# Hymba encoder block on one core: other tile places at the end of each up stage, and an addition of the second up stage held behind a weight split

## The chip, the cores and the metric

The kernel runs on one core of one Trainium2 chip. The metric is the device time of one execution in microseconds (us). The engines have these names: PE is TensorE (matmuls; PEld its weight loads), ACT is ScalarE, DVE is VectorE, POOL is GpSimd and SP is SyncE. POOL and SP mostly issue transfers here, each into a queue of its own.

## The reference

A layer of an encoder over 2,048 tokens and 16 learned meta tokens, width 1,024, all in float32. An attention group and a Fourier group stand side by side, then comes an MLP, then a last norm:

```
h = concat(meta, x)
hn = rms_norm(h, g_mix); proj = hn @ w_in
mixed = concat(rms_norm(attention(q, k, v)), rms_norm(fourier_mix(u)))
h = h + mixed @ w_out
m = rms_norm(h, g_mlp)
h = h + square(relu(m @ w_up)) @ w_down        # w_up 1024 x 4096, w_down 4096 x 1024
return rms_norm(h, g_final)[:, n_meta:]
```

The change touches the MLP alone, the last two lines but one.

## The kernel before, in words

**Splitting.** Every float32 matrix goes to TensorE as two parts in the type fp32r: a high part, a cast on ACT (L70), and a low part, source minus high part, on DVE (L71). Together they are called a split. A product takes three matmuls of 128x512 (`mm3`, L80 to L82): high by high, high by low, low by high.

**Seven forms.** The MLP's two products are done in 2x2 blocks with seven block products in place of eight, named by digits and done in the order 1, 2, 6, 5, 7, 3, 4. Some operands are sums or differences of blocks, which DVE works out. Results of several forms are added up into the blocks of the product.

**Two passes, two stages each.** The tokens are taken in two passes, p = 0 and p = 1. Each pass has an up stage (`up_pass`) and a down stage (`down_pass`).

- Up stage: eight groups g of 512 hidden columns; for each, seven forms of 24 matmuls into two banks each. The activation parts are the tiles `bf` (in the first pass made in place, in the second read back from memory, 2 MB for a form: L1616, L1622). The raw weights are `R0` and `R1`, their sums `us1` and `us2` (L1138, L1139, L1144), their parts `wuh` and `wul`. After form 2, ACT has copied form 1's result out (`p1`, L1248) and DVE adds the two halves `c11` (L1259); ACT then applies relu and square (L1212, L1213). The results and their sums `s1` to `s4` are stored to memory, `s_d`, from SP's queue (L1219).
- Down stage: four groups of seven forms of 48 matmuls. The stored results come back as raws `a` (L1351), the weights w_down as raws `d11`, `d21`, `d12`, `d22` (L1332); in the first group both are issued by POOL. DVE works out the sums of weights (L1372: `d11`, `t2` and so on). Parts of activations are `ah`, `al`, parts of weights `bh`, `bl`. Form 1's parts for the first group (`a1p`, `bh1`, `bl1`, `ah1`, `al1`) are made in the up stage, by `first_down`. Results lie in four banks `dx` and four banks `dy`; DVE adds them to the residual `hs` (L1493). Form 6 writes into the `dx` banks again, after form 1's additions have read them.

**What sets the order.** TensorE's order is the order of the code. For the other engines a layer that records the program sets it, mostly in the order in which inputs are there; `tc.issue_after(x)` puts what it encloses behind instruction x. Every wait comes from the data or from addresses: SBUF is shared out by pools at the left and the right end (`dn` left and `dr` right for the down stage, `pc` and `sp` right in the up stage, `bfb` left in the second up stage). A pool takes the addresses of one that was released, and with `reuse_waits="tile"` a new tile waits for exactly those instructions that still read or write the old tile at its place. `place` sets in which order the tags of a pool take their addresses. `own2` makes the parts of form 2 in places of their own, `ah0` to `bl1`; all other parts take turns in rings, "a" in `dn` and "b" in `dr`.

At the end of the up stage `sp` is released after form 1's matmuls are in the queue, and `dr` lies where it was, so over the tiles `R0`, `us1`, `us2`, which hold form 1's parts at that time:

```
if "b" not in RING:
    sp.release()
    if final_pass:
        wup.release()
    dr = right(f"dr{p}")
    RING["b"] = dr, b_bufs
    place(dr, ("b", 1024, b_bufs))
    own2("b", 0)
```

Of the kernel before, what the change touches and what calls it, by code (L numbers as in the profile page):

```python
# [12 lines left out]
R32 = mybir.dt.float32r  # L13
AF = mybir.ActivationFunctionType
ALU = mybir.AluOpType
# [4 lines left out]
P = 128  # L20
# [64 lines left out]
def ins_of(x):  # L85
    return getattr(x, "ins", x)
# [49 lines left out]
def encoder_block(ctx: ExitStack, tc: tile.TileContext, x, meta, w_in, w_f,  # L136
                  w_out, w_up, w_down, g_fin, g_cols, g_rows, c_id, c_rope, c_dft, c_even, c_odd, c_rem, out):
    nc = tc.nc
    split = Split(nc)
    x = x[0]  # L140
# [451 lines left out]
    for j in range(LAST + 1):  # L592
# [16 lines left out]
        else:  # L609
# [14 lines left out]
            a = 0  # L624
# [578 lines left out]
                load(*items[at + 1])  # L1203
            yield

    def up_pass(p, sp, pc, UW, ready, first, hs, beside):

        def c_tile(name):
            return pc.tile([P, 512], F32, name=f"{name}_{p}", tag="c", bufs=11)
# [5 lines left out]
        for g in range(8):  # L1215
# [5 lines left out]
            for name in ORDER:  # L1221
# [21 lines left out]
                for q in range(2):  # L1243
                    nm = f"{g}_{q}"
                    if name in "165":
                        d = p1 if name == "1" else u2 if name == "6" else p5
                        d[q] = pc.tile([P, 512], F32, name=f"p{name}_{p}_{nm}", tag="p", bufs=P_BUFS)
                        nc.scalar.copy(d[q], (Y if name == "5" else X)[q])  # L1248
                    elif name == "4":
                        C["21", q] = c = c_tile("c21_" + nm)  # L1250
                        relu2(c, X[q])
                        keep("2", q, c)
                        s4 = c_tile("s4_" + nm)
                        nc.vector.tensor_tensor(s4, c, C["s2", q], op=ALU.subtract)
                        keep("3", q, s4)
                    else:
                        f, a, b = {"2": ("11", Y, p1), "7": ("22", X, p5), "3": ("12", Y, u2)}[name]
                        C[f, q] = c = c_tile(f"c{f}_{nm}")
                        nc.vector.tensor_tensor(c, a[q], b[q], op=ALU.add)  # L1259
                        relu2(c, c)  # L1260
                        if name != "3":
                            keep("1" if name == "2" else "4", q, c)
                        else:
                            s1, s2, s3 = (c_tile(f"s{i}_{nm}") for i in (1, 2, 3))
                            nc.vector.tensor_tensor(s1, c, C["22", q], op=ALU.add)
                            keep("5", q, s1)
                            nc.vector.tensor_tensor(s2, s1, C["11", q], op=ALU.subtract)
                            keep("6", q, s2)
                            C["s2", q] = s2
                            nc.vector.tensor_tensor(s3, C["11", q], c, op=ALU.subtract)  # L1270
                            keep("7", q, s3)
# [32 lines left out]
    def down_pass(p, sp, FIRST, hs):  # L1304

        dn = left(f"dn{p}")
        final_pass = p == 1
        own, RING = {}, {"a": (dn, 8)}
        a_bufs, b_bufs = (5, 10) if p else (4, 8)

        def place(pool, *tags):

            for tag, cols, bufs in tags:
                pool.tile([P, cols], F32, name=f"z{tag}_{p}", tag=tag, bufs=bufs)

        raws_ = {n: (n, 1024, 2) for n in ("d11", "d21", "d12", "d22", "t2")}
        ends_ = [(n, 512, 1) for n in ("gf0", "gf1", "ej0", "ej1")]
        own_ = [(n, 1024, 1) for n in ("ah0", "al0", "ah1", "al1")]
        if p:
            place(dn, *ends_, *(raws_[n] for n in ("t2", "d21", "d11")), ("ar", 1024, a_bufs), *own_,  # L1320
                  raws_["d12"], raws_["d22"], ("a", 1024, 8))
        else:
            place(dn, raws_["d11"], raws_["d21"], ("ar", 1024, a_bufs), *own_, raws_["d12"], raws_["d22"], raws_["t2"],
                  ("a", 1024, 8), *ends_)

        def load(raw, g, i, j):
            raw[i, j] = []
# [7 lines left out]
        def own2(x, g):  # L1335

            for h in range(2):
                own[g, x, h] = [RING[x][0].tile([P, 2, 512], R32, name=f"{x}{e}2_{p}_{g}_{h}", tag=f"{x}{e}{h}")
                                for e in "hl"]

        def down_operands():
# [87 lines left out]
        ready = [next(DO)]  # L1429
# [42 lines left out]
        for g in range(4):  # L1472
            X, Y = {}, {}
            last = g == 3
            for name in ORDER:
# [36 lines left out]
                if not (last and name == "4"):  # L1512
                    for t in range(4):
                        products(t)
# [3 lines that stand above are left out]
                            wup.release()  # L1518
                        dr = right(f"dr{p}")
                        RING["b"] = dr, b_bufs  # L1520
                        place(dr, ("b", 1024, b_bufs))
                        own2("b", 0)
                        ready.append(next(DO))
                    w = next(DO, None)
                    if w is not None:
# [28 lines left out]
    sp = right("sp0")  # L1554
    UW = up_weights(0, sp, sp)
    ready = [next(UW), next(UW)]
# [42 lines left out]
    pc = right("pc0")  # L1599
    hs, FIRST = [], []  # L1600
# [5 lines left out]
    ready = down_pass(0, sp, FIRST, hs)  # L1606
    sp = right("sp1")
    spr = left("spr1")
    UW = up_weights(1, sp, spr)
# [7 lines left out]
    for name in "2U65734":  # L1617
        with tc.issue_after(ins_of(behind)):
            if name == "U":
                ready.append(next(UW))  # L1620
            else:
                behind = nc.sync.dma_start(f32v(BT[name]), f_d[name])  # L1622
    pc = right("pc1")
    hs, FIRST = [], []
    up_pass(1, sp, pc, UW, ready, first_down(1, FIRST, sp), hs, iter(()))
    pc.release()
    bfb.release()
    spr.release()
# [103 lines left out]
```

## Time and profile before

| | |
|---|---|
| median of 3 runs | 2271.43 us (2271.02 to 2275.55) |
| profiled execution | 2272.19 us |
| its span, first to last instruction | 2270.4 us |
| mean granted TensorE clock | 0.997 |
| PE busy | 2240.4 us, 99% |
| DVE busy | 1693.0 us, 75% |
| ACT busy | 1177.8 us, 52% |

In the rows of the profile "dx<-bh,ah" names the written tile and the read ones by the program's names, with the numbers of form and group left out; where several tiles share a line, the first name stands for all (the row "c<-uy,p" is the addition at L1259). In brackets stands how long the engine had stood idle just before the instruction and what ended that. A row of the timeline is: start, duration (or, for a group of "xN" instructions in a row, their time together), engine, line, operation. Matmul times overlap: one starts about every 0.227 us and lasts 0.39. The first down stage begins at 1332.07 us, the second up stage at 1641.7, the second down stage at 1954.22.

### The profile page before, as it was taken

The numbers are of one execution on the slowest core, as the hardware profiler recorded it, in microseconds if no ns is written. First come the engines' busy times: TensorE is split into PE (matmuls) and PEld (weight loads), VectorE is DVE, ScalarE is ACT, GpSimd is POOL, SyncE is SP. The second block draws the span as 40 slices with busy tenths as digits, with TensorE's granted clock in tenths as the row PEclk, the third lists the DMA queues.
The fourth block names the chain that finished last, engine by engine and source line by source line (L and its number), as shares of the span: only waits on it lengthen the run. The fifth ranks groups of instructions, "written<-read, shape, count | busy, mean of one in ns | idle before, by whom it ended". The sixth has DMA issues, their size and how long they took to land.

```text
span 2270.4 us, 28121 instructions
## 1 busy us (share of the span) xinstructions
PE 2240.4 (99%) x10238; PEld 1774.5 (78%) x10238; DVE 1693.0 (75%) x2250; ACT 1177.8 (52%) x1997; POOL 248.0 (11%) x285
## 2 busy tenths in 40 slices
PE   9999999999999999999999999999999999999998
PEld 7888987766667666677888878888878888788887
DVE  6334589999999888888676669679655656696795
ACT  6443366665555566668555644334445555443343
POOL 2212120003223122010000020000200000200000
PEclk9999999999999999999999999999999999999999
DMA  5332252133343524367777575444674444864442
GB/s 203 89 107 77 78 157 81 51 94 113 101 155 116 192 90 136 126 254 243 254 233 237 201 275 192 158 133 149 227 311 166 156 151 155 306 201 157 128 138 84
DMA packets 191786, 367.40 MB, mean 162 GB/s; under 512 B 15760, under 2 KB 74768, under 8 KB 189984
## 3 DMA queue, kind: packets, MB, share of 16 engines
q1 hardware_dynamic: 171040, 310.08, 40.4%
q0 software_dynamic: 20464, 55.27, 7.7%
q8 instruction: 80, 1.31, 0.2%
q14 instruction: 58, 0.48, 0.1%
q10 hardware_dynamic: 144, 0.26, 0.0%
HBM read 236.28 MB, written 129.27 MB: 161 GB/s over the span
## 4 chain that ended last, share of the span: by engine, by line
PE 88%; DVE 7%; ACT 2%; issue 2%; POOL 1%; DMA 1%; POOLq 0%; DVEq 0%; ACTq 0%; SPq 0%
PE o L849 7%; PE ux L82 5%; PE ux L80 5%; PE ux L81 5%; PE dx L80 5%; PE dx L81 5%; PE dx L82 5%; PE uy L82 4%; PE uy L81 4%; PE uy L80 4%; PE dy L82 4%; PE dy L80 4%; PE dy L81 4%; PE s L80 2%; PE s L82 2%; PE s L81 2%
## 5 line engine op out<-in xcount | busy, mean ns | idle before, releaser
L849 PE MATMUL o<-S,vn 128*128 128x512 f32 x512 | 243.6, 596 | 4.2 <-ACT S L841 3.5
L70 ACT CAST ah<-a 128x1024 fp32r<-128x1024 f32 x108 | 112.9, 1050 | 259.8 <-PE dx L81 105.3
L80 PE MATMUL dx<-bh,ah 128*128 128x512 f32 x496 | 192.6, 388 | 1.3 <-DVE hs L1493 1.3
L780 ACT COPY S<-s 128x512 f32<-128x512 f32 x256 | 145.0, 584 | 91.9 <-PE s L82 72.5
L82 PE MATMUL dx<-bh,al 128*128 128x512 f32 x496 | 192.5, 388 | 0.0
L81 PE MATMUL dx<-bl,ah 128*128 128x512 f32 x496 | 192.5, 388 | 0.0
L80 PE MATMUL ux<-bf,wuh 128*128 128x512 f32 x448 | 176.0, 393 | 3.2 <-ACT wuh L70 3.1
L82 PE MATMUL ux<-bf,wul 128*128 128x512 f32 x448 | 175.4, 392 | 0.7 <-DVE wul L71 0.7
L81 PE MATMUL ux<-bf,wuh 128*128 128x512 f32 x448 | 175.4, 391 | 0.0
L840 DVE TENSOR_TENSOR S<-S,mb 128x1024 f32<-128x1024 f32 x128 | 155.2, 1227 | 11.8 <-ACT mb L811 11.7
L841 ACT ACTIVATE S<-S 128x1024 f32<-128x1024 f32 x128 | 135.1, 1063 | 43.3 <-DVE S L840 42.2
L80 PE MATMUL dy<-bh,ah 128*128 128x512 f32 (+1 forms) x388 | 151.5, 390 | 3.5 <-ACT ah L70 3.5
L82 PE MATMUL dy<-bh,al 128*128 128x512 f32 (+1 forms) x388 | 151.3, 390 | 1.6 <-DVE al L71 1.6
L71 DVE TENSOR_TENSOR al<-a,ah 128x1024 fp32r<-128x1024 f32 x108 | 131.1, 1220 | 27.2 <-ACT ah L70 26.9
L81 PE MATMUL dy<-bl,ah 128*128 128x512 f32 (+1 forms) x388 | 151.2, 390 | 0.0
L849 PEld LDWEIGHTS o<-S,vn 128*128 128x128 f32 x512 | 92.2, 189 | 75.1 <-issue 59.0
L80 PE MATMUL s<-q,kt 128*128 128x512 f32 (+1 forms) x272 | 145.1, 534 | 2.8 <-ACT S L780 2.4
L71 DVE TENSOR_TENSOR bl<-d,bh 128x1024 fp32r<-128x1024 f32 x92 | 112.1, 1219 | 21.5 <-ACT bh L70 21.5
L80 PE MATMUL uy<-bf,wuh 128*128 128x512 f32 x320 | 125.0, 391 | 0.3 <-ACT wuh L70 0.3
L82 PE MATMUL uy<-bf,wul 128*128 128x512 f32 x320 | 124.6, 390 | 0.7 <-DVE wul L71 0.7
L786 DVE TENSOR_TENSOR M<-M,S 128x1024 f32<-128x1024 f32 x96 | 117.6, 1225 | 9.9 <-ACT S L780 9.0
L81 PE MATMUL uy<-bf,wuh 128*128 128x512 f32 x320 | 124.8, 390 | 0.0
(323 smaller groups left out, 5663.2 us busy)
## 6 DMA issues: line engine op xcount, KB each, us to landing
a<-s_d SPq DMA_DIRECT2D x84, 512.0 KB, 3.7
R<-in_w_up_dram SPq DMA_DIRECT2D x32, 1024.0 KB, 5.5
s_d<-s SPq DMA_DIRECT2D x128, 256.0 KB, 2.1
s_d<-c SPq DMA_DIRECT2D x96, 256.0 KB, 2.8
d<-in_w_down_dram SPq DMA_DIRECT2D x48, 512.0 KB, 5.1
f_d<-lf SPq DMA_DIRECT2D x56, 256.0 KB, 2.8
bf<-f_d SPq DMA_DIRECT2D x7, 2048.0 KB, 13.5
a<-s_d POOLq DMA_DIRECT2D x24, 512.0 KB, 5.3
```

What stands on the lines that cost most here:

```text
L70: self.high = nc.scalar.copy(hi, src)
L71: self.low = nc.vector.tensor_tensor(lo, src, f32v(hi), op=ALU.subtract)
L80: nc.tensor.matmul(out, a[0], b[0], start=first, stop=False, skip_group_check=chain)
L81: nc.tensor.matmul(out, a[0], b[1], start=False, stop=False, skip_group_check=chain)
L82: nc.tensor.matmul(out, a[1], b[0], start=False, stop=last, skip_group_check=chain)
L780: nc.scalar.copy(S[:, i % 2], ps)
L786: nc.vector.tensor_tensor(M, M, S, op=ALU.max)
L840: nc.vector.tensor_tensor(S, S, mb, op=ALU.subtract)
L841: nc.scalar.activation(p, S, AF.Exp, scale=ISQ)
L849: nc.tensor.matmul(s["O"], v[:, 2 * j % 4 + e], p[:, e], start=i + e == 1, stop=False)
```

## The change

Three edits, with no instruction added or removed.

1. **Own places of form 2's weight parts** (`bh0`, `bl0`, `bh1`, `bl1`). In the second pass they move from `dr` to `dn`, behind `d22` and ahead of the ring "a". In the first pass they stay in `dr`, but take its first addresses, ahead of the ring "b".
2. **First pass, order in `dn`:** the ring "a" takes its addresses ahead of `d12`, `d22` and `t2`, no longer behind them.
3. **Second pass, first group:** the additions of `c11` after form 2 are issued behind the split of form 6's weights (`held`).

```diff
--- before.py
+++ after.py
@@ -1203,7 +1203,7 @@
                 load(*items[at + 1])
             yield
 
-    def up_pass(p, sp, pc, UW, ready, first, hs, beside):
+    def up_pass(p, sp, pc, UW, ready, first, hs, beside, held=None):
 
         def c_tile(name):
             return pc.tile([P, 512], F32, name=f"{name}_{p}", tag="c", bufs=11)
@@ -1256,7 +1256,8 @@
                     else:
                         f, a, b = {"2": ("11", Y, p1), "7": ("22", X, p5), "3": ("12", Y, u2)}[name]
                         C[f, q] = c = c_tile(f"c{f}_{nm}")
-                        nc.vector.tensor_tensor(c, a[q], b[q], op=ALU.add)
+                        with tc.issue_after(held) if held is not None and (g, name) == (0, "2") else nullcontext():
+                            nc.vector.tensor_tensor(c, a[q], b[q], op=ALU.add)
                         relu2(c, c)
                         if name != "3":
                             keep("1" if name == "2" else "4", q, c)
@@ -1316,12 +1317,13 @@
         raws_ = {n: (n, 1024, 2) for n in ("d11", "d21", "d12", "d22", "t2")}
         ends_ = [(n, 512, 1) for n in ("gf0", "gf1", "ej0", "ej1")]
         own_ = [(n, 1024, 1) for n in ("ah0", "al0", "ah1", "al1")]
+        ownb_ = [(n, 1024, 1) for n in ("bh0", "bl0", "bh1", "bl1")]
         if p:
             place(dn, *ends_, *(raws_[n] for n in ("t2", "d21", "d11")), ("ar", 1024, a_bufs), *own_,
-                  raws_["d12"], raws_["d22"], ("a", 1024, 8))
+                  raws_["d12"], raws_["d22"], *ownb_, ("a", 1024, 8))
         else:
-            place(dn, raws_["d11"], raws_["d21"], ("ar", 1024, a_bufs), *own_, raws_["d12"], raws_["d22"], raws_["t2"],
-                  ("a", 1024, 8), *ends_)
+            place(dn, raws_["d11"], raws_["d21"], ("ar", 1024, a_bufs), *own_, ("a", 1024, 8), raws_["d12"],
+                  raws_["d22"], raws_["t2"], *ends_)
 
         def load(raw, g, i, j):
             raw[i, j] = []
@@ -1335,7 +1337,7 @@
         def own2(x, g):
 
             for h in range(2):
-                own[g, x, h] = [RING[x][0].tile([P, 2, 512], R32, name=f"{x}{e}2_{p}_{g}_{h}", tag=f"{x}{e}{h}")
+                own[g, x, h] = [(dn if final_pass else RING[x][0]).tile([P, 2, 512], R32, name=f"{x}{e}2_{p}_{g}_{h}", tag=f"{x}{e}{h}")
                                 for e in "hl"]
 
         def down_operands():
@@ -1518,8 +1520,8 @@
                             wup.release()
                         dr = right(f"dr{p}")
                         RING["b"] = dr, b_bufs
+                        own2("b", 0)
                         place(dr, ("b", 1024, b_bufs))
-                        own2("b", 0)
                         ready.append(next(DO))
                     w = next(DO, None)
                     if w is not None:
@@ -1618,11 +1620,12 @@
         with tc.issue_after(ins_of(behind)):
             if name == "U":
                 ready.append(next(UW))
+                held = ins_of(split.low)
             else:
                 behind = nc.sync.dma_start(f32v(BT[name]), f_d[name])
     pc = right("pc1")
     hs, FIRST = [], []
-    up_pass(1, sp, pc, UW, ready, first_down(1, FIRST, sp), hs, iter(()))
+    up_pass(1, sp, pc, UW, ready, first_down(1, FIRST, sp), hs, iter(()), held)
     pc.release()
     bfb.release()
     spr.release()
```

Lines behind L1258 have a number higher by one after the change, and by two to three further down (L1332 is L1334, L1351 is L1353, L1493 is L1495, L1622 is L1625).

The order on TensorE is the same before and after. On the other engines order and waits differ, above all at three places. In the rows that follow a name such as `bh2_0_0_1` gives form 2, pass 0, group 0, half 1. The brackets name the counters waited for: PE is TensorE's, DMAHW those of SP's transfers, DMASW those of POOL's.

**First down stage, ACT.** Behind the last results of the up stage (`c21_7`) come the casts of form 2's parts. Before:

```order
L1212 ACTIVATE c21_7_1_0_11778<-ux_0_7_1_11503 128x512 [waits DMAHW6_49,DMAHW2_49,PE_49]
L1213 ACTIVATE c21_7_1_0_11778<-c21_7_1_0_11778 128x512 [waits Activation_49]
L70 CAST bh2_0_0_0_11898<-d21_0_0_0_11807 128x1024 [waits DMASW5_49]
L70 CAST bh2_0_0_1_11900<-d21_0_0_1_11809 128x1024 [waits DMASW6_49,PE_49]
L70 CAST ah2_0_0_0_11821<-a2_0_0_0_11815 128x1024 [waits DMASW1_49]
L70 CAST ah2_0_0_1_11823<-a2_0_0_1_11817 128x1024 [waits DMASW2_49]
L70 CAST bh6_0_0_0_11945<-t2_0_0_0_11819 128x1024 [waits DVE_49]
```

After, the second cast has one counter less:

```order
L1212 ACTIVATE c21_7_1_0_11778<-ux_0_7_1_11503 128x512 [waits DMAHW6_49,DMAHW2_49,PE_49]
L1213 ACTIVATE c21_7_1_0_11778<-c21_7_1_0_11778 128x512 [waits Activation_49]
L70 CAST bh2_0_0_0_11897<-d21_0_0_0_11807 128x1024 [waits DMASW5_49]
L70 CAST bh2_0_0_1_11899<-d21_0_0_1_11809 128x1024 [waits DMASW6_49]
L70 CAST ah2_0_0_0_11821<-a2_0_0_0_11815 128x1024 [waits DMASW1_49]
L70 CAST ah2_0_0_1_11823<-a2_0_0_1_11817 128x1024 [waits DMASW2_49]
L70 CAST bh6_0_0_0_11945<-t2_0_0_0_11819 128x1024 [waits DVE_49]
```

The second cast (`bh2_0_0_1`) waited for TensorE, for the last matmul of form 1; now it waits for its raw alone. At the second down stage the same two casts, `bh2_1_0_0` and `bh2_1_0_1`, both lose such a wait; there `bl2_1_0_1` on DVE now waits for the end of the up stage.

**First down stage, POOL.** The loads of form 6's raws (`d12`, `d22`, `a6`) and of form 5's (`a5`). Before:

```order
L1332 DMA d11_0_0_1_11813<-in_w_down_dram 128x2x512 [waits DMAHW4_49,DMAHW5_49,DMAHW1_49,DMASW0_49]
L1351 DMA a2_0_0_0_11815<-s_d0_8865 128x1024 [waits DMAHW0_49,DMAHW2_49,DMASW1_49,PE_49]
L1351 DMA a2_0_0_1_11817<-s_d0_8865 128x1024 [waits DMAHW5_49,DMAHW2_49,DMASW2_49]
L1332 DMA d12_0_0_0_11910<-in_w_down_dram 128x2x512 [waits DMASW3_49,DVE_49,Activation_49]
L1332 DMA d12_0_0_1_11912<-in_w_down_dram 128x2x512 [waits DMASW4_49,Activation_49]
L1332 DMA d22_0_0_0_11914<-in_w_down_dram 128x2x512 [waits DMASW5_49]
L1332 DMA d22_0_0_1_11916<-in_w_down_dram 128x2x512 [waits DMAHW3_49,DMAHW4_49,DMAHW2_49,DMAHW5_49,DMAHW1_49,DMAHW6_49,DMAHW0_49,DMAHW7_49,DMASW6_49,DVE_49]
```

After, the first load has the long list, and the fourth a short one:

```order
L1334 DMA d11_0_0_1_11813<-in_w_down_dram 128x2x512 [waits DMAHW4_49,DMAHW5_49,DMAHW1_49,DMASW0_49]
L1353 DMA a2_0_0_0_11815<-s_d0_8865 128x1024 [waits DMAHW0_49,DMAHW2_49,DMASW1_49,PE_49]
L1353 DMA a2_0_0_1_11817<-s_d0_8865 128x1024 [waits DMAHW5_49,DMAHW2_49,DMASW2_49]
L1334 DMA d12_0_0_0_11910<-in_w_down_dram 128x2x512 [waits DMAHW3_49,DMAHW2_49,DMAHW4_49,DMAHW1_49,DMAHW5_49,DMAHW0_49,DMAHW6_49,DMASW3_49,DMAHW7_49,DVE_49,PE_49]
L1334 DMA d12_0_0_1_11912<-in_w_down_dram 128x2x512 [waits DMASW4_49]
L1334 DMA d22_0_0_0_11914<-in_w_down_dram 128x2x512 [waits DMAHW4_49,DMAHW3_49,DMAHW7_49,DMAHW1_49,DMASW5_49]
L1334 DMA d22_0_0_1_11916<-in_w_down_dram 128x2x512 [waits DMASW6_49]
```

The long wait has moved from the fourth load to the first, which now waits for stores of the up stage, the last of them that of `c21_7_0_0`, and for TensorE. The loads behind it each wait for fewer counters, and no longer for ACT or DVE until `a5`.

**Second up stage, DVE.** Form 2's additions (`c11`), the sums `us1`, `us2` and the low parts `wul`. Before:

```order
L1458 SCALAR_TENSOR_TENSOR hs0_1_11930<-hs0_1_11930,ers_0_7_14081,gf0_0_11935 128x512 [waits Pool_49]
L1259 TENSOR_TENSOR c11_0_0_1_14192<-uy2_1_0_0_14161,p1_1_0_0_14157 128x512 [waits PE_49,Activation_49]
L1138 TENSOR_TENSOR us1_1_0_14111<-R0_1_0_14107,R1_1_0_14109 128x1024 [waits DMAHW3_49,DMAHW2_49]
L1259 TENSOR_TENSOR c11_0_1_1_14197<-uy2_1_0_1_14174,p1_1_0_1_14159 128x512 [waits PE_49,Activation_49]
L1139 TENSOR_TENSOR us2_1_0_14112<-us1_1_0_14111,R0_1_0_14107 128x1024 [waits DVE_49]
L1142 TENSOR_TENSOR R0_1_0_14107<-R0_1_0_14107 128x4x256 [waits DVE_49]
L71 TENSOR_TENSOR wul6_1_0_14116<-us2_1_0_14112,wuh6_1_0_14115 128x1024 [waits Activation_49]
L71 TENSOR_TENSOR wul5_1_0_14154<-us1_1_0_14111,wuh5_1_0_14153 128x1024 [waits Activation_49]
L71 TENSOR_TENSOR wul7_1_0_14189<-R0_1_0_14107,wuh7_1_0_14188 128x1024 [waits Activation_49]
L1144 TENSOR_TENSOR us2_1_0_14112<-R1_1_0_14109,us2_1_0_14112 128x1024 [waits DVE_49]
```

After, the sums come first, and the additions behind three low parts:

```order
L1460 SCALAR_TENSOR_TENSOR hs0_1_11930<-hs0_1_11930,ers_0_7_14081,gf0_0_11935 128x512 [waits Pool_49]
L1138 TENSOR_TENSOR us1_1_0_14111<-R0_1_0_14107,R1_1_0_14109 128x1024 [waits DMAHW3_49,DMAHW2_49]
L1139 TENSOR_TENSOR us2_1_0_14112<-us1_1_0_14111,R0_1_0_14107 128x1024 [waits DVE_49]
L1142 TENSOR_TENSOR R0_1_0_14107<-R0_1_0_14107 128x4x256 [waits DVE_49]
L71 TENSOR_TENSOR wul6_1_0_14116<-us2_1_0_14112,wuh6_1_0_14115 128x1024 [waits Activation_49]
L71 TENSOR_TENSOR wul5_1_0_14154<-us1_1_0_14111,wuh5_1_0_14153 128x1024 [waits PE_49,Activation_49]
L71 TENSOR_TENSOR wul7_1_0_14189<-R0_1_0_14107,wuh7_1_0_14188 128x1024 [waits PE_49,Activation_49]
L1260 TENSOR_TENSOR c11_0_0_1_14192<-uy2_1_0_0_14161,p1_1_0_0_14157 128x512
L1260 TENSOR_TENSOR c11_0_1_1_14197<-uy2_1_0_1_14174,p1_1_0_1_14159 128x512
L1144 TENSOR_TENSOR us2_1_0_14112<-R1_1_0_14109,us2_1_0_14112 128x1024 [waits DVE_49]
```

Both additions now stand behind the low parts of forms 6, 5 and 7; the sums are the first to run. The low part of form 5 now waits for a matmul of form 2 as well, that of form 7 for one of the last of form 2.

**Second up stage, SP.** The loads of `R` and `bf`. Before:

```order
L1616 DMA bf1_14099<-f_d1_133 128x4096 [waits PE_49]
L1622 DMA bf2_14098<-f_d2_134 128x4096 [waits DMAHW6_49,DMAHW5_49,DMAHW7_49,DMAHW4_49,DVE_49]
L1128 DMA R0_1_0_14107<-in_w_up_dram 128x4x512
L1128 DMA R1_1_0_14109<-in_w_up_dram 128x4x512
L1622 DMA bf6_14100<-f_d6_135 128x4096
L1622 DMA bf5_14101<-f_d5_136 128x4096 [waits PE_49]
L1622 DMA bf7_14104<-f_d7_137 128x4096 [waits DMASW3_49,DMASW4_49,DMASW2_49,DMASW5_49,DMASW1_49,DMASW6_49,DMASW0_49,DMASW7_49,DVE_49,Activation_49]
L1622 DMA bf3_14102<-f_d3_138 128x4096 [waits PE_49]
L1622 DMA bf4_14103<-f_d4_139 128x4096 [waits DMAHW0_49,DVE_49,Activation_49]
```

After, the order is the same and three waits differ:

```order
L1618 DMA bf1_14099<-f_d1_133 128x4096 [waits PE_49]
L1625 DMA bf2_14098<-f_d2_134 128x4096 [waits DMAHW6_49,DMAHW5_49,DMAHW7_49,DMAHW4_49,DVE_49]
L1128 DMA R0_1_0_14107<-in_w_up_dram 128x4x512
L1128 DMA R1_1_0_14109<-in_w_up_dram 128x4x512
L1625 DMA bf6_14100<-f_d6_135 128x4096 [waits PE_49]
L1625 DMA bf5_14101<-f_d5_136 128x4096 [waits PE_49]
L1625 DMA bf7_14104<-f_d7_137 128x4096 [waits DMASW3_49,DMASW4_49,DMASW2_49,DMASW5_49,DMASW1_49,DMASW6_49,DMASW0_49,DMASW7_49,DVE_49,Activation_49]
L1625 DMA bf3_14102<-f_d3_138 128x4096
L1625 DMA bf4_14103<-f_d4_139 128x4096 [waits DMAHW0_49,DVE_49,Activation_49]
```

`bf6`'s load now waits for TensorE, for the matmul for which `bf5`'s waited before; `bf5`'s waits for one of seven matmuls later, and `bf3`'s no longer waits for TensorE.

## The prediction

> **What bounds the kernel now.** The page comes first. TensorE is busy almost throughout:
>
> ```profile
> span 2270.4 us, 28121 instructions
> PE 2240.4 (99%) x10238; PEld 1774.5 (78%) x10238; DVE 1693.0 (75%) x2250; ACT 1177.8 (52%) x1997; POOL 248.0 (11%) x285
> ```
>
> So a gain must come from TensorE's idle time or from matmuls that run slowly. The edit adds no instruction and leaves TensorE's order alone. The table of waits on TensorE says where it stands still (us in total, times, longest):
>
> ```profile
> PE dy L80 <- ACT ah L70: 3.5, 2, 2.1
> PE ux L80 <- ACT wuh L70: 3.1, 1, 3.1
> PE dy L82 <- DVE al L71: 1.6, 2, 0.9
> PE dx L80 <- DVE hs L1493: 1.3, 1, 1.3
> ```
>
> Those four groups, 9.5 us, lie at three places: the start of the first down stage, the start of the second up stage, and the start of the second down stage. TensorE's timeline there (start, duration, wait in brackets):
>
> ```profile
> 1332.07 0.39 PE L80 MATMUL dx<-bh,ah 128*128 128x512 f32 x1
> ...
> 1342.72 0.39 PE L82 MATMUL dx<-bh,a1p 128*128 128x512 f32 x1
> 1345.19 0.50 PE L80 MATMUL dy<-bh,ah 128*128 128x512 f32 x1 [2.08 <-ACT ah L70]
> ...
> 1358.68 0.47 PE L80 MATMUL dx<-bh,ah 128*128 128x512 f32 x1 [1.31 <-DVE hs L1493]
> ...
> 1652.33 0.39 PE L82 MATMUL uy<-bf,wul 128*128 128x512 f32 x1
> 1655.83 0.80 PE L80 MATMUL ux<-bf,wuh 128*128 128x512 f32 x1 [3.11 <-ACT wuh L70]
> ...
> 1664.59 0.39 PE L80 MATMUL uy<-bf,wuh 128*128 128x512 f32 x1
> ...
> 1964.87 0.39 PE L82 MATMUL dx<-bh,a1p 128*128 128x512 f32 x1
> 1966.71 0.50 PE L80 MATMUL dy<-bh,ah 128*128 128x512 f32 x1 [1.45 <-ACT ah L70]
> ...
> 1980.53 0.39 PE L80 MATMUL dx<-bh,ah 128*128 128x512 f32 x1
> ```
>
> The first two rows are the first and the last of 48 matmuls: (1342.72 − 1332.07) / 47 = 0.2267 us from one to the next. With this pitch I price each place start to start, which takes the slow matmuls in. The table by stretches shows those (length, busy us and count of PE, PEld, DVE, ACT and POOL, then clock, DMA share, GB/s):
>
> ```profile
> 1345.20:1353.00 7.80, 7.08 (x30) 5.55 (x31) 7.80 (x8) 2.73 (x3) 4.21 (x8) 1.00 0.94 333
> 1655.80:1662.00 6.20, 6.12 (x14) 4.34 (x15) 4.65 (x5) 2.10 (x3) 0.00 (x0) 0.50 1.02 433
> 1969.60:1973.20 3.60, 3.60 (x10) 2.83 (x10) 3.60 (x4) 0.33 (x1) 3.23 (x7) 0.56 0.91 278
> ```
>
> Behind two of the three places the granted clock is at half; behind the first it stays at 1.00.
>
> **Term 1, start of the first down stage.** The product after dx is form 2's; it waits for its weight and activation parts. Before, the second weight cast sits on an address that dx still reads:
>
> ```profile
> 1343.14 1.04 ACT L70 CAST bh<-d 128x1024 fp32r<-128x1024 f32 x1 [8.67 <-PE dx L82]
> ...
> 1345.37 2.35 DVE L71 TENSOR_TENSOR al<-a,ah 128x1024 fp32r<-128x1024 f32 x2
> 1347.64 2.35 DVE L1372 TENSOR_TENSOR d<-d,d 128x1024 f32<-128x1024 f32 x2
> ...
> 1357.86 2.47 DVE L1493 TENSOR_TENSOR hs<-hs,dx 128x512 f32<-128x512 f32 x4
> ```
>
> ScalarE was free from 1343.14 − 8.67 = 1334.47. Queued behind that cast are the two `ah` casts, and on VectorE the `bl`, both `al`, the weight sums of form 6 and the `hs` additions that empty dx's banks; form 6, which writes those banks, waits for these last. Normal: form 2's 48 matmuls follow dx directly, form 6 begins at 1342.72 + 49 × 0.2267 = 1353.83. It began at 1358.68: 4.85 us lost.
>
> After: the casts no longer wait for dx. `bh` runs 1334.5 to 1335.5, both `ah` (about 1 each, as that cast) to about 1337.4, both `al` (a step of 1.14 each) to about 1339.2, before dx ends at 1342.95. What is late next is the raws of form 6, whose queue the edit also moves:
>
> ```profile
> 1329.53 2.17 POOL L1332 DMA_DIRECT2D d<-in_w_down_dram  x3 [12.20 <-ACT c L1212]
> 1342.41 0.72 POOL L1332 DMA_DIRECT2D d<-in_w_down_dram  x1 [10.71 <-issue]
> 1332.67 0.63 SPq L1219 DMA_DIRECT2D s_d<-c  x1
> s_d<-c SPq DMA_DIRECT2D x1, 256.0 KB, 8.3
> s_d<-c SPq DMA_DIRECT2D x96, 256.0 KB, 2.8
> d<-in_w_down_dram POOLq DMA_DIRECT2D x1, 512.0 KB, 4.1
> ```
>
> Before, three raw loads went out at 1329.5 and the fourth waited behind a store of the up stage until 1342.41. After, all four wait for an up-stage store issued at 1332.67, and POOL holds the form-6 and form-5 activation loads behind them. That store took 8.3 us while the three loads were in flight, the median is 2.8. Without those loads before it I take the median: landed 1335.5, four issues of 0.72 until 1338.4, the first raw there at 1335.5 + 4.1 = 1339.6. From the first weight sum to the end of the first `hs` addition VectorE took 1357.86 + 0.6 − 1347.64 = 10.8 us without a gap; from 1339.6 it ends at 1350.4, 3.4 us ahead of 1353.83. **Gain 4.85**; at 8.3 us the raw lands at 1345.1, form 6 begins at about 1355.9, gain 2.8; with slower raws too (rival C) less.
>
> **Term 2, start of the second up stage.** After product 2, product 6 waits for its weight part:
>
> ```profile
> 1650.11 0.69 DVE L1259 TENSOR_TENSOR c<-uy,p 128x512 f32<-128x512 f32 x1 [2.94 <-PE uy L82]
> 1650.72 1.22 DVE L1138 TENSOR_TENSOR us<-R,R 128x1024 f32<-128x1024 f32 x1
> 1654.75 1.98 ACT L70 CAST wuh<-us 128x1024 fp32r<-128x1024 f32 x2
> 1623.39 0.98 SPq L1128 DMA_DIRECT2D R<-in_w_up_dram  x2
> R<-in_w_up_dram SPq DMA_DIRECT2D x1, 1024.0 KB, 16.6
> ```
>
> VectorE stood from 1647.17 for the first half of product 2, which its first addition (L1259) needs; then came one weight sum, then the second addition, which needs the other half, then the second sum, and ScalarE squared in between. The raws had landed at about 1623.9 + 16.6 = 1640.5. After, both additions stand behind three weight splits: sums 1647.2 to 1649.5, cast to about 1650.6, split to about 1651.9, before 1652.56. Product 6's 24 matmuls then end normally, and form 5 starts at 1652.33 + 25 × 0.2267 = 1658.00. It started at 1664.59: **6.59 us**, of which 1655.83 − 1652.56 = 3.27 is the wait, and 1664.59 − 1655.83 − 24 × 0.2267 = 3.32 the half clock.
>
> Late next: the two additions end near 1656.2, after the split of form 7 (its cast waits for the end of product 2), and ScalarE does its four squares after its three casts; the copies of product 6 follow by about 1660.4, the product that reuses those banks starts at 1663.4. That is covered by product 6. Then the activation parts, since the edit also moves their waits:
>
> ```profile
> 1640.29 0.34 SPq L1622 DMA_DIRECT2D bf<-f_d  x1
> 1650.19 0.40 SPq L1622 DMA_DIRECT2D bf<-f_d  x1
> bf<-f_d SPq DMA_DIRECT2D x1, 2048.0 KB, 22.0
> bf<-f_d SPq DMA_DIRECT2D x1, 2048.0 KB, 13.5
> bf<-f_d SPq DMA_DIRECT2D x1, 2048.0 KB, 21.2
> ```
>
> Form 6's load (22.0) was issued directly behind R's two, at 1624.4, with 6 MB ahead of it, and landed at 1646.4; form 5's (13.5) went out at 1640.29, when TensorE was done with an older part. Now form 6's waits for that point, and form 5's goes out about 1.5 us later. R landed near 1640.5 and form 6's part 5.9 us behind it, so after a 1640.29 issue I estimate 5.9 + 1 to 2, landed at 1647.2 to 1648.2; needed at 1652.56. Its bounds are the two other rows: 13.5 gives 1653.8, 1.2 us late; 22.0 gives 1662.3, 9.7 late. The row nearest is neither, as both queued behind other parts. Form 5's should land near 1655 (needed 1658.0). The fourth of these rows, form 4's, landed at 1650.19 + 21.2 = 1671.4, and its product now begins at 1674.3.
>
> **Term 3, start of the second down stage.** The same two casts:
>
> ```profile
> 1963.71 2.00 ACT L70 CAST bh<-d 128x1024 fp32r<-128x1024 f32 x2 [8.03 <-PE dx L81]
> ```
>
> ScalarE was free from 1955.68. Normal start of form 6: 1964.87 + 49 × 0.2267 = 1975.98; it was 1980.53: **4.55 us** (1.45 and, by the table of waits, 0.9 of waits; the other 2.2 are the half clock and the first matmuls behind a wait). After: casts from about 1955.7 to 1959.6, both `al` by about 1961, then 10.8 us of sums, splits and the first addition to about 1972, before 1975.98. POOL's loads are not moved here. So the gain is all of it; the lower bound is nothing, if another wait has the same end.
>
> **Sum.** 4.85 + 6.59 + 4.55 = 16.0. The profiled execution took 2272.19 us (1.8 around its span), so 2256.2; the median shown is 0.76 below it, so **2255.4**.
>
> [...] In the second up stage half clock follows a wait of 3.11, in the second down stage waits of 1.45 and 0.9, in the first none follows 2.08. [...]
>
> **Rivals.**
> - **B, a part of x is late.** Form 6's `bf` load takes form 5's 13.5: +1.2 us, and with a slow stretch behind that wait as in term 3 +2.2 more: 2256.6 to 2258.8. For: the memory engines are at a share of 1.02 or more there, and TensorE now asks 6.6 us earlier for all later parts. Against: form 6's margin of 4.4 us or more, and the total traffic is the same.
> - **C, the raws of the first down stage are late.** The store takes its 8.3 us, and the raw like form 2's neighbours longer: term 1 shrinks to between 2.8 and nothing: 2257.5 to 2260.3. For: the 8.3 row. Against: the three loads in front of it are gone.
> - **D, the slow stretches stay.** They follow a clock of their own and not these waits; then 3.32 + 2.2 stay: 2260.9. For: a wait of 2.08 us in the first down stage brought none. Against: both stand directly behind a wait.
> - **E, slower than before.** Form 6's load, now issued 16 us later, lands late enough to eat everything. At its own 22.0 us TensorE waits 9.7, with 3.3 at half clock: 13.0 of the 16.0 go, 2268.4. Each further us is lost one to one: no gain at 25.0 us, and slower by 4.5 from 29.5 us, which is 2275.9. For: loads there took up to 22 us. Against: those had three or four parts queued ahead of them.
> - **F, a part of the change does nothing** (a place still has its old wait): term 2 stays, 2262.0; terms 1 or 3 stay, 2260.
>
> **How the numbers follow.** My forecast (A) 0.68; B 0.12, C 0.06, D 0.05, E 0.05, F 0.04. The likeliest gives 2255.4. The range, 2253.0 to 2261.5, reaches 2.4 below for the start-to-start terms and the spread between runs (2271.02 to 2275.55), and above to D and to most of F. No-change means within 0.2%, or 4.5 us, of 2271.43, what a measurement of this kernel can tell. Faster: A to D and F are all under 2266.9, and so is the short end of E; 0.92 after a part of every case is set aside for what no row shows. Of E 0.03 is slower, the rest is counted as the same, 0.05.
>
> **What would show it.** In the table of waits the four groups shrink to under 1 us in sum; the clock is 1.00 behind the starts of all three stages; form 6 of the first down stage begins 21.8 us after the first dx matmul (now 26.6), form 5 of the second up stage 5.67 after product 2's last matmul (now 12.26), form 6 of the second down stage 11.1 after dx's last (now 15.66). POOL's four raw loads go out in one run about 3.4 us after dx begins. If `ux` waits for a DMA instead, B or E holds; if dx's form 6 still waits for `hs`, C; half clock without a wait, D.

## The result

| | before | changed |
|---|---|---|
| median | 2271.69 us (6 runs, 2271.02 to 2275.55) | 2257.70 us (6 runs, 2255.64 to 2260.33) |
| profiled execution | 2272.19 us | 2255.64 us |
| its span | 2270.4 us | 2253.6 us |

The ratio is 0.9935, with a 95% interval from 0.9922 to 0.9947. The change is faster by 14.0 us in the median; the forecast was 2255.4 us in a range from 2253.0 to 2261.5.

The table of waits on TensorE in the changed kernel (us in total, times, longest):

```profile
PE o L849 <- ACT S L841: 3.4, 5, 1.6
PE s L80 <- ACT S L780: 2.0, 4, 0.8
PE pwake L216 <- DVE wake L213: 1.5, 1, 1.5
...
PE ux L82 <- DVE wul L71: 0.7, 1, 0.7
PE uy L82 <- DVE wul L71: 0.7, 1, 0.7
```

The four groups that the prediction names (3.5, 3.1, 1.6 and 1.3 us) are gone, and no new wait of more than 0.8 us has come in. Apart from 0.7 us at a later group of the second up stage, what is left lies ahead of 1031 us, in parts that the change does not touch. TensorE's timeline at the three places, in the changed kernel:

```profile
1331.51 0.39 PE L80 MATMUL dx<-bh,ah 128*128 128x512 f32 x1
...
1342.16 0.39 PE L82 MATMUL dx<-bh,a1p 128*128 128x512 f32 x1
1342.39 0.39 PE L80 MATMUL dy<-bh,ah 128*128 128x512 f32 x1
...
1353.27 0.39 PE L80 MATMUL dx<-bh,ah 128*128 128x512 f32 x1
...
1646.80 0.39 PE L82 MATMUL uy<-bf,wul 128*128 128x512 f32 x1
1647.03 0.39 PE L80 MATMUL ux<-bf,wuh 128*128 128x512 f32 x1
...
1652.47 0.39 PE L80 MATMUL uy<-bf,wuh 128*128 128x512 f32 x1
...
1952.74 0.39 PE L82 MATMUL dx<-bh,a1p 128*128 128x512 f32 x1
1952.97 0.39 PE L80 MATMUL dy<-bh,ah 128*128 128x512 f32 x1
...
1963.85 0.39 PE L80 MATMUL dx<-bh,ah 128*128 128x512 f32 x1
```

One matmul follows another at 0.23 us at each of the joints. From start to start, as the prediction priced it:

| place | before | changed | gain | forecast |
|---|---|---|---|---|
| first down stage, first dx to form 6 | 26.61 | 21.76 | 4.85 | 4.85 |
| second up stage, last of product 2 to form 5 | 12.26 | 5.67 | 6.59 | 6.59 |
| second down stage, last dx to form 6 | 15.66 | 11.11 | 4.55 | 4.55 |

The table by stretches of the changed kernel (length, busy us of PE, PEld, DVE, ACT, POOL, then clock, DMA share, GB/s) shows full clock behind all three:

```profile
1342.30:1360.00 17.70, 17.70 (x80) 14.66 (x79) 17.62 (x20) 7.83 (x8) 4.80 (x9) 1.00 1.02 395
1647.00:1660.00 13.00, 13.00 (x59) 10.74 (x58) 6.38 (x7) 7.50 (x11) 0.00 (x0) 1.00 1.01 427
1952.90:1970.00 17.10, 17.10 (x78) 14.14 (x77) 17.10 (x20) 8.64 (x9) 2.13 (x4) 1.00 0.97 365
```

So the profile, which is that of the fastest of the six executions, confirms every term to the hundredth, and yet the median stands 2.3 us above the forecast, and the six runs spread over 4.7 us. The six runs of the kernel before spread over 4.5 us. That is what the experiments ask about. How close the new order comes to its next limits is read from the rows that answer to those of before (timelines of the changed kernel; in the last three, what was loaded and its us from issue to landing):

```profile
1335.36 2.89 POOL L1334 DMA_DIRECT2D d<-in_w_down_dram  x4 [18.57 <-DVE bl L71]
1340.41 1.23 DVE L1374 TENSOR_TENSOR d<-d,d 128x1024 f32<-128x1024 f32 x1 [1.83 <-DMA d<-in_w_down_dram]
1351.26 2.47 DVE L1495 TENSOR_TENSOR hs<-hs,dx 128x512 f32<-128x512 f32 x4
...
1641.56 1.22 DVE L1138 TENSOR_TENSOR us<-R,R 128x1024 f32<-128x1024 f32 x1
1649.23 1.28 DVE L1260 TENSOR_TENSOR c<-uy,p 128x512 f32<-128x512 f32 x2
1673.33 1.04 ACT L70 CAST wuh<-R 128x1024 fp32r<-128x1024 f32 x1
...
bf<-f_d SPq DMA_DIRECT2D x1, 2048.0 KB, 9.9
bf<-f_d SPq DMA_DIRECT2D x1, 2048.0 KB, 25.9
R<-in_w_up_dram SPq DMA_DIRECT2D x1, 1024.0 KB, 18.7
```

In the first down stage the four raws go out together at 1335.36; VectorE waits 1.83 us for the first and ends the first `hs` addition near 1351.9, which leaves 1.4 us to form 6. In the second up stage form 6's `bf`, its part of the input x, (9.9) was issued at 1634.76 and landed at 1644.7, 2.3 us ahead of its use; form 4's (25.9), issued at 1641.7, landed 1.2 us ahead; the second group's first R (18.7), issued at 1652.87, landed at 1671.6, 1.7 us ahead of its cast at 1673.33.

### The profile page after: what moved, and what is told of

Its sections match the earlier page's. It is cut to its first block, busy times and chain, and to the rows that moved or that the text cites. A ratio compares the mean times of both kernels' runs of the same rounds, so it can differ in the third digit from the quotient of the medians.

```text
span 2253.6 us, 28116 instructions
## 1 busy us (share of the span) xinstructions
PE 2233.3 (99%) x10238; PEld 1771.3 (79%) x10238; DVE 1692.9 (75%) x2250; ACT 1178.1 (52%) x1997; POOL 247.8 (11%) x285
## 4 chain that ended last, share of the span: by engine, by line
PE 89%; DVE 5%; ACT 2%; DMA 1%; issue 1%; POOL 1%; SPq 0%; POOLq 0%; ACTq 0%; DVEq 0%
PE o L849 7%; PE ux L82 5%; PE ux L80 5%; PE ux L81 5%; PE dx L82 5%; PE dx L81 5%; PE dx L80 5%; PE dy L82 4%; PE dy L81 4%; PE dy L80 4%; PE uy L82 4%; PE uy L80 4%; PE uy L81 4%; PE s L80 2%; PE s L82 2%; PE s L81 2%
## 5 line engine op out<-in xcount | busy, mean ns | idle before, releaser
L1212 ACT ACTIVATE c<-c 128x512 f32<-128x512 f32 x96 | 60.5, 631 | 119.4 <-DVE c L1260 116.6
```

The lines of the kernel that those rows point to most:

```text
L1212: nc.scalar.activation(dst, src, AF.Relu)
```

## The experiments

Two questions: are the three places independent, and what costs the median 2 us? For the second the first theory (T1) was the loads of `bf` with their small margins, the rival (T2) the raws of the first down stage. The kernel before ran beside each set: 2272.48 us (15 runs), 2272.91 (9) and 2272.87 (9) in the median.

**The held additions alone (e1).** The kernel before with the third edit alone, shown here by its core; `held` is set and handed on as in the change:

```diff
-                        nc.vector.tensor_tensor(c, a[q], b[q], op=ALU.add)
+                        with tc.issue_after(held) if held is not None and (g, name) == (0, "2") else nullcontext():
+                            nc.vector.tensor_tensor(c, a[q], b[q], op=ALU.add)
```

> The kernel before with the third edit alone (the additions of c11 held). Own theory: the three places are independent, so the second up stage gives its 6.6 us and nothing else changes: about 2265.1 us against 2271.7, runs within about 1 us of each other, since form 6's load is still issued early, right behind R. Rival (a slow clock of its own): the 3.3 us of half clock stay, about 2268.4. In the profile the wait of ux on wuh (3.1) is gone, the down stages' waits (2.1, 1.45, 0.9, 1.3) stay.

2267.75 us in the median of 11 runs (2265.29 to 2270.76), ratio 0.9981 [0.9972, 0.9990]. **The places without it (e2)**, that is, the change with `held` left out of the second call of `up_pass`:

```diff
-    up_pass(1, sp, pc, UW, ready, first_down(1, FIRST, sp), hs, iter(()), held)
+    up_pass(1, sp, pc, UW, ready, first_down(1, FIRST, sp), hs, iter(()))
```

> The change without its third edit (places moved, additions not held). Own theory: both down stages give 4.85 + 4.55 = 9.4 us: about 2262.3. What the runs of the changed kernel spread over (2255.6 to 2260.3) is, by theory T1, the loads of bf, which land 1.0 to 2.3 us ahead of their use in its fastest run; here TensorE still loses 6.6 us at that place, the loads have that much more slack, and the runs should lie within about 1 us. By rival T2 the spread comes from the raws of the first down stage, which this kernel has too (VectorE waited 1.8 us for them, with 1.3 us left): then the runs spread over 3 us or more here as well.

2262.09 us (5 runs, 2261.10 to 2262.58), ratio 0.9952 [0.9940, 0.9965]. By medians the two parts give 4.7 and 10.4 us, together 15.1, which is what the whole change gave on the same chip (2257.41): they add up, but the split is not the forecast one, 6.6 and 9.4. By stages, in one profile of each, it is: the second up stage takes 305.94 us in e1 (312.54 before, the half clock gone with the wait), both down stages are as before, and e2 is the mirror image; the table of stages below has the rows. e2 speaks against T2: its five runs lie within 1.5 us though it has the same raws in the first down stage.

The clock explains 0.7 us of e2's surplus, in its one profile. e2 keeps the wait of 3.11 us, but TensorE's timeline and the stretch behind it show half clock for about 3.3 us (0.50 in the 3.2 us of the last row) where that of the kernel before lasted 6.8 (0.50 from 1655.32 to 1662.14):

```profile
1647.14 0.39 PE L82 MATMUL uy<-bf,wul 128*128 128x512 f32 x1
1650.64 0.50 PE L80 MATMUL ux<-bf,wuh 128*128 128x512 f32 x1 [3.11 <-ACT wuh L70]
...
1658.66 0.39 PE L80 MATMUL uy<-bf,wuh 128*128 128x512 f32 x1
...
1652.50:1655.70 3.20, 3.20 (x9) 2.49 (x8) 2.76 (x3) 0.00 (x0) 0.00 (x0) 0.50 1.00 424
```

From product 2 to form 5 that is 11.52 us, not 12.26. Why e1 falls 1.9 us short of its 6.6 in the median is not shown: its 11 runs spread over 5.5 us, and its profile, of the fastest of them, has the whole gain. In e1's clock it is the first down stage, untouched there, that differs:

```profile
1344.89 0.50 PE L80 MATMUL dy<-bh,ah 128*128 128x512 f32 x1 [2.08 <-ACT ah L70]
...
1358.51 0.40 PE L80 MATMUL dx<-bh,ah 128*128 128x512 f32 x1
...
1346.50:1349.80 3.30, 3.30 (x9) 2.56 (x10) 3.30 (x4) 0.00 (x0) 2.60 (x5) 0.51 0.82 274
```

The same wait of 2.08 us as before, and here half clock follows it. It costs almost nothing: form 6 begins 26.74 us after the first dx matmul (1331.77), 0.13 more than before, as it had 1.3 us to wait for `hs` anyway.

**Form 6's load early again (e3).** The changed kernel with another order of the parts' places:

```diff
-    for name in "2165347":
+    for name in "2153647":
```

> The changed kernel with another order of the bf tiles in their pool, so that form 6's place is one that is free early and forms 5 and 3 take the places that the first pass's last matmuls read; form 6's load is issued right behind R again, some 16 us earlier. T1 (late bf loads make the changed kernel's runs 0 to 4.7 us slower than its fastest): median about 2255.5, runs within about 1.5 us. T2 (raws of the first down stage): nothing changes, median about 2257.7, spread over 4 us.

2257.52 us (5 runs, 2256.37 to 2261.73): no difference, and no narrower. **The changed kernel again (e4):**

> The changed kernel once more, for more runs and a second profile. All theories: about 2257.7, from 2255.6 to 2260.3. If the profile falls on a slower execution it tells T1 and T2 apart: T1 a wait of ux or uy in the second up stage for a transfer of bf, or for what follows it; T2 a wait of form 6 (dx) for hs in the first down stage, on account of the raws.

2257.41 us (5 runs, 2256.20 to 2259.81). Its profile fell on a quick execution (2256.20 us) without either wait. T1 in its first form, form 6's late load, falls with e3. The form that remained was T3: all loads there together are only just quick enough, and slower executions wait for them. Its rival is T4: the spread has nothing to do with these loads.

**Less traffic in the second up stage (e5).** The last 8 stores of the first pass's output wait behind the first group's results, on SP's queue. The edit is shown in part; the lines that issue what `LATE` holds are left out:

```diff
-                eng.dma_start(out[(8 * p + t) * P:(8 * p + t + 1) * P, halves[h]], w)
+                go = lambda eng, h=h, w=w: eng.dma_start(out[(8 * p + t) * P:(8 * p + t + 1) * P, halves[h]], w)
+                LATE.append(go) if not final_pass and t >= 4 else go(eng)
```

> The changed kernel; the last 8 of the first pass's 16 stores of the output (2 MB) go out behind the first group's results in the second up stage instead of among the loads of bf. Nothing else moves. Theory T3 (with the wait gone, TensorE in the second up stage uses up 2 MB of bf in 5.44 us, about as fast as the 16 DMA engines bring it, and executions in which transfers are a few per cent slower lose 1 to 5 us there): 2 MB at 400 GB/s are 5.2 us, so the parts land that much earlier and the runs come together, median about 2255.8, slowest under 2258. Rival T4 (the spread has nothing to do with these transfers): median 2257.5, spread 3.5 us or more, as before.

2256.81 us (5 runs, 2255.05 to 2257.52). **More traffic (e6),** four copies from memory to memory behind the stores, also shown in part (`x_d` is scratch memory that nothing reads):

```diff
-                eng.dma_start(out[(8 * p + t) * P:(8 * p + t + 1) * P, halves[h]], w)
+                d = ins_of(eng.dma_start(out[(8 * p + t) * P:(8 * p + t + 1) * P, halves[h]], w))
+            if not final_pass and t >= 4:
+                i = t - 4
+                with tc.issue_after(d):
+                    nc.gpsimd.dma_start(x_d[i], f_d["1"][:, i // 2, i % 2 * 2:i % 2 * 2 + 2])
```

> The changed kernel with 2 MB more traffic in the same stretch: four copies of 512 KB from memory to memory, queued behind the last stores of the first pass's output; the result doesn't use them. T3: the parts of bf land 5 us later than in the changed kernel, of which the 1 to 1.4 us of slack are used first; TensorE waits for bf in the second up stage, 3 to 5 us in all, median about 2261 to 2263, and the profile shows waits of ux or uy on a transfer. T4: 2257.5, no such wait.

2262.41 us (5 runs, 2260.96 to 2262.84), 5 us slower than the changed kernel, as expected in size. The place was expected only in part. TensorE's and ScalarE's timelines, and the landing of the second group's R:

```profile
1670.35 0.47 PE L80 MATMUL ux<-bf,wuh 128*128 128x512 f32 x1 [0.30 <-DMA bf<-f_d]
1679.51 0.79 PE L80 MATMUL ux<-bf,wuh 128*128 128x512 f32 x1 [3.45 <-ACT wuh L70]
...
1678.41 1.04 ACT L70 CAST wuh<-R 128x1024 fp32r<-128x1024 f32 x1 [3.77 <-DMA R<-in_w_up_dram]
...
R<-in_w_up_dram SPq DMA_DIRECT2D x1, 1024.0 KB, 24.5
```

The parts of x cost 0.30 us. What is late is the next group's weights, queued behind them, which none of the prediction's steps looked at: 3.45 us of wait, with matmuls of 0.79 us behind it. So the margin is real and as small as the rows say, and 2 MB more use it up.

**The change without its second edit (e7):**

```diff
-            place(dn, raws_["d11"], raws_["d21"], ("ar", 1024, a_bufs), *own_, ("a", 1024, 8), raws_["d12"],
-                  raws_["d22"], raws_["t2"], *ends_)
+            place(dn, raws_["d11"], raws_["d21"], ("ar", 1024, a_bufs), *own_, raws_["d12"], raws_["d22"], raws_["t2"],
+                  ("a", 1024, 8), *ends_)
```

> The changed kernel without its second edit (in the first pass the ring a lies behind d12, d22 and t2 again). Form 2's casts are free as in the changed kernel; POOL's three raw loads go out at 1329.5 again and the fourth waits for a store until about 1342. Own theory: the fourth raw lands at 1346.5 and form 6's activations at 1348.5 to 1349, so the chain on VectorE ends near 1353.7, just when form 6 wants to start: 0 to 1 us of term 1 is lost, about 2257.7 to 2258.7. Rival: the second edit carries most of term 1; form 6 starts 3 us late or more, about 2260.5.

2256.39 us (5 runs, 2255.83 to 2257.50). POOL's, VectorE's and TensorE's timelines:

```profile
1331.03 2.17 POOL L1334 DMA_DIRECT2D d<-in_w_down_dram  x3 [12.20 <-ACT c L1212]
1343.75 0.72 POOL L1334 DMA_DIRECT2D d<-in_w_down_dram  x1 [10.55 <-DVE d L1374]
...
1353.77 2.47 DVE L1495 TENSOR_TENSOR hs<-hs,dx 128x512 f32<-128x512 f32 x4
...
1355.32 0.39 PE L80 MATMUL dx<-bh,ah 128*128 128x512 f32 x1
```

The fourth raw is as late as it was before the change, and form 6 still begins without a wait, 21.76 us after the first dx matmul (1333.56). All of term 1 comes from the first edit; the second only moves the slack.

**The edits of e5 and e3 together (e8):**

> The deferred stores together with form 6's load right behind R. T3: as with the stores deferred alone, with more slack still: median about 2255.5, runs within 1.5 us. T4: 2257.5 with the spread of the changed kernel.

2257.09 us (5 runs, 2256.35 to 2258.75): nothing added.

**Side by side on one chip.** The set above ran on another chip than the changed kernel, so its smaller spread proved little. The changed kernel (f1), e5's kernel (f2), e7's kernel (f3), and both edits (f4):

> The changed kernel again, as the yardstick for the runs beside it, which are on the same chip. T3 (transfers in the second up stage land just in time: bf4 and the second group's R 1.2 to 1.8 us ahead of their use, so that slower executions wait there): median 2257.4, slowest near 2260. T4 (the runs of every kernel spread this much): the same, and the runs beside it as wide.

> The changed kernel with 8 of the 16 stores of the first pass's output behind the first group's results, again, now beside the changed kernel on one chip. T3: about 1 us under it in the median (2256.5), the slowest run 2 us under its slowest. T4: no difference that can be told.

> The changed kernel without its second edit, again, now beside the changed kernel on one chip. Form 6's part of x is loaded right behind R as before the change, form 6 of the first down stage starts in time all the same (0.9 us of slack). Theory: equal to the changed kernel or up to 1 us faster, 2256.4 to 2257.4. Rival (the second edit is worth something): 1 us or more slower, 2258.4.

> Both together: 8 stores deferred, second edit left out. T3: most slack of all for the loads of the second up stage, median about 2256, runs within 2 us. T4: as the changed kernel, 2257.4.

| | median of 5 | range |
|---|---|---|
| f1 changed kernel | 2257.57 | 2257.42 to 2259.46 |
| f2 stores deferred | 2256.10 | 2255.29 to 2258.25 |
| f3 without the second edit | 2258.01 | 2254.94 to 2258.71 |
| f4 both | 2257.15 | 2255.70 to 2259.92 |

Their ranges overlap. f2's median is 1.5 us below f1's, as T3 expected, but f4, which by T3 has the most slack, spreads widest. What settled it was that f1's profile fell on one of the longer executions (2258.93 us, 3.3 more than the first profile of the same program). From the first matmul of each stage in each profile, by subtraction; the last stage is taken to the end of the span, which is known to 0.1 us, and the execution lasts 1.7 to 2.0 us longer than the span:

| profile | first dx at | first down | second up | second down, to the span's end | execution |
|---|---|---|---|---|---|
| before | 1332.07 | 309.61 | 312.54 | 316.18 | 2272.19 |
| changed | 1331.51 | 304.64 | 305.94 | 311.51 | 2255.64 |
| e1 held alone | 1331.77 | 309.64 | 305.94 | 316.15 | 2265.29 |
| e2 places alone | 1331.85 | 304.64 | 311.79 | 311.62 | 2261.62 |
| e6 more traffic | 1332.52 | 304.63 | 310.47 | 311.58 | 2260.96 |
| e7 no second edit | 1333.56 | 304.64 | 305.94 | 311.56 | 2257.50 |
| f1 changed, again | 1335.08 | 304.63 | 305.94 | 311.55 | 2258.93 |
| f2 deferred, again | 1334.35 | 304.63 | 305.95 | 311.47 | 2258.25 |

The stages that the change touches repeat to 0.1 us in every profile of a kernel with the first and the third edit, e3, e4, e5, e8, f3 and f4 among them, only e6 with its copies apart. T2's raws are in the first down stage, which takes 304.63 or 304.64 us in short and long executions alike. All of f1's 3.3 us lie ahead of the first dx matmul, in stages that the change doesn't touch: up to the raw loads at the end of the first up stage every engine's instructions stand in the same order in the profiles of both kernels. The waits, TensorE's timeline and a stretch in the attention part of f1, and the same stretch of the changed kernel's first profile:

```profile
PE o L849 <- ACT S L841: 4.3, 5, 2.4
...
519.43 3.65 PE L849 MATMUL o<-S,vn 128*128 128x512 f32 x4 [2.43 <-ACT S L841]
...
500.00:550.00 50.00, 46.56 (x168) 29.46 (x167) 46.16 (x56) 33.29 (x61) 14.04 (x13) 0.97 0.44 144
```

```profile
517.89 1.98 PE L849 MATMUL o<-S,vn 128*128 128x512 f32 x4 [1.61 <-ACT S L841]
...
500.00:550.00 50.00, 47.07 (x175) 29.84 (x174) 48.51 (x57) 34.78 (x62) 16.17 (x15) 1.00 0.47 149
```

A wait that is there in both is 0.8 us longer in f1, and half clock follows it (four matmuls take 3.65 us, not 1.98, and the mean clock of the stretch is 0.97, not 1.00). Set beside the first profile matmul by matmul, f1 is 0.7 us behind at 515 us and 3.2 us behind at 522, so this place makes 2.5 of the 3.6 us by which its first dx comes later. It is not the same place each time: f2 and f3, 2.8 and 2.3 us later, lose 1.9 and 1.4 us between 1100 and 1260 us, in the first up stage. T3 falls as the cause of the spread, and T4 holds: in no profile of a kernel with the held additions, but for e6 with its copies, did the second up stage take longer than 305.96 us.

## Why the prediction was right, and where it missed

- **What bounds the kernel**, TensorE's idle time at three joints and the half clock behind two of them: right, by the waits that vanished and by e1 and e2, each of which cured its own places alone. The prediction's table of waits leaves out rows that stand between its four (3.5, 2.4 and 1.5 us, all ahead of 980 us); the change left those alone, so nothing hung on them.
- **How far the three terms are tested.** Each term is all the time lost at its place, so it comes out to the hundredth as soon as no wait is left there. What the profile tests is that none is; the margins behind the terms are a harder test, and there the steps were less good.
- **Term 1, 4.85:** measured 4.85. The store landed in 2.4 us (median taken: 2.8). The margin behind it was put at 3.4 us and is 1.4: counted from the first dx the four raws went out 0.4 us later than forecast, the first of them took 5.0 us and not 4.1, and the chain on VectorE took 11.5 us and not 10.8, in part because its second weight sum had to wait again for a raw. By e7 the moved raw loads, on which this step spent most of its words, were not needed for the gain.
- **Term 2, 6.59:** measured 6.59, the half clock with it. Form 6's part took 9.9 us from its issue, not the 7 to 8 estimated, so its margin was 2.3 us and not 4.4 or more. The step left out the next group's R behind it, where e6 lost most.
- **Term 3, 4.55:** measured 4.55.
- **Rivals.** B and C did not happen; e6 shows what late loads cost there once traffic grows, 4.5 us in that stage with 2 MB, most of it for weights and not, as in B, for a part of x. D is wrong here: wherever the waits went, the half clock went (1.00 behind all three places in the changed kernel). E would have needed a load of 25 us where 9.9 was measured. F is excluded by the table of places.
- **From the sum to the median:** this is the step that was mis-sized. 16.0 was expected to be the difference of the medians; all runs of the two kernels give 2272.53 (39 runs) and 2257.47 (16 runs), 15.1 apart, and the first six of each 14.0. The stages gave 16.2 in the two profiles. The step took the part ahead of the change for as long as in one profiled execution of before (first dx at 1332.07), while profiles of the changed program alone have it from 1331.51 to 1335.08, and the lost time in the second up stage at 6.6, while e2's execution lost 5.85 there, with the shorter half-clock stretch. How much of the missing 1 to 2 us is the one and how much the other stays open: the profiles are single executions, and only one of the kernel before was taken apart.

None of the variants beats the changed kernel by more than the runs scatter. The deferred stores have the lowest median (2256.3 of 10 runs against 2257.47 of 16), but their stage times are the same, so the difference cannot be placed.

## What to carry to other kernels

Where nothing is added and TensorE's order stays, price a stall from the start of the last matmul before it to the start of the next product it delays: that takes in both the wait and the slow clock behind it, and here it was right to 0.01 us between two profiled executions. The slow clock behind a stall differs between executions (5.85 or 6.6 us for the same stall), so one profile gives one draw of it. A stall that closes brings later loads forward (here the second group's first R went out at 1652.87 us, before at 1659.34); follow the queue to its end, past the loads of this group to the next group's weights. And before a shortfall of 1 to 2 us is explained by the change, take the profiles apart by stages: the spread was in stages that the change never touched.

## What the runs showed of the hardware that was not expected

Half clock followed a wait in one execution and not in another. TensorE's waits in the profiles, with the granted clock at their end and behind it (for the attention part, the mean of a longer stretch around the wait):

| profile | wait, with its end | clock |
|---|---|---|
| before | 3.11 to 1655.83 | 0.50 from 1655.32 to 1662.14, full on both sides |
| e2 | 3.11 to 1650.64, 0.54 to 1651.91 | 0.50 from 1652.50 to 1655.70 |
| before | 2.08 to 1345.19, 0.72 to 1346.64 | 1.00 from 1345.20 to 1353.00 |
| e1 | 2.08 to 1344.89 | 0.51 from 1346.50 to 1349.80 |
| before | 1.45 to 1966.71, 0.91 to 1968.35 | 0.50 from 1969.34 to 1972.76, full on both sides |
| before | 1.68 to 517.28 | 1.00 from 515.00 to 525.00 |
| changed | 1.61 to 517.89 | 1.00 from 500.00 to 550.00 |
| f1 | 2.43 to 519.43 | 0.97 from 500.00 to 550.00 |

So in these traces the length of a wait does not tell what follows: 2.08 us brought half clock in e1 and none in the kernel before, where 1.45 and 0.91 us did, and behind the same 3.11 us it lasted 6.8 us before and about 3.3 us in e2.

In the profile of the kernel before, the clock drops at 1655.32, at 1969.34 and, behind the last matmul, at 2266.30 us. The distances, 314.03 and 296.96 us, are 92 and 87 times 3.413 us, the length of the shorter of the two stretches above. In the 3.41 us ahead of the first two drops, matmuls were busy for 0.82 and 1.72 us. The wait of 2.08 us falls into two such steps, counted from the drops, 1341.30 to 1344.71 and 1344.71 to 1348.12, with matmuls busy for 1.81 and 2.21 us, and that of 1.68 us into one, 515.30 to 518.71, with 1.73 us; behind all three the clock stayed at 1.00. An estimate from these five numbers: what counts is the time without matmuls in one step, so that a wait divided between two can pass. In e1 the clock was low from 1346.50 us on, and the 3.41 us ahead of that hold 1.8 of its 2.08 us. The five are from one profile (the ends of matmuls in it are modelled), and no run was made to test it.
